# Two first weight tiles taken row by row, gate columns beside the last value columns, two query and key tiles inside memory attention

## The chip, the cores and the metric

The kernel runs on one core of a Trainium2 chip. A time is the device time of one execution in microseconds (us); lower is better. The engines are named as the profile names them: PE is TensorE (matmuls and transposes; PEld its weight loads), ACT is ScalarE, DVE is VectorE, POOL is GpSimd, SP is SyncE, which here only issues transfers (DMA). Each engine works through its own instructions in order and waits at semaphores for the others.

## The reference, cut to what matters

Two layers of a transformer on 512 tokens of width 1024, each a mixer with memory attention beside it and then a convolutional feed-forward block. The change lies in the projections of the first layer, whose mixer is gated linear attention (GLA):

```python
xn = rmsnorm(h, norm_mix[i])                       # x * rsqrt(mean(x*x) + eps) * gain
mem_kv = rmsnorm(mem, norm_mem[i]) @ w_mem_kv[i]   # 256 memory tokens
q, k, v, g, lr, mq = split_cols(xn @ gla_w_in[i], GLA_SIZES)   # 384, 384, 768, 768, 16, 256
log_a = jax.nn.log_sigmoid((lr @ gla_w_gate_up[i] + gla_b_gate[i])) / GLA_GATE_NORM
main = gla_mixer(q, k, v, log_a, g, gla_out_norm[i])
mo = mem_attention(mq, mem_kv)
h = h + jnp.concatenate([main, mo], axis=-1) @ w_out[i]
```

The 16 columns of lr are the gate columns: the decays log_a come from them.

## The kernel before

Activations lie transposed: the 1024 features are eight tiles (k = 0 to 7) of 128 partitions by 512 tokens. Every number is carried as a high and a low part (xh, xl; wh, wl; Qh, Ql), and each product is three matmuls: high by high, low by high, high by low. The high part is written by ScalarE (L277, L280 or L263), the low part, a difference, by VectorE (L278, L281 or L264). Weights come in tiles of 128 by 1024 (512 KB) over SyncE's queue (L243) into a pool of three buffers (wraw), and their parts into pools of three (wh, wl).

The row scale (the rsqrt of the mean square) isn't put on x. Projections take x times gain, and the scale is multiplied in afterwards. It is made of eight squares (ACT) summed on VectorE (sqacc, L332), a sum over partitions on TensorE (L338), a small VectorE step (rc, L348), a power on GpSimd (L349), and four transposes (L355) that spread it over partitions; ScalarE copies it out (rb, L359). For the memory tokens the same is done under names with m: rows mt (three buffers), parts mh and ml, sums sqaccm, scale rcm and rbm.

The order of the first layer before. The first key tile (glak[0]) comes in two halves, between rows of x. It is multiplied as rows arrive (L525), 24 matmuls, and between them stand three groups of fp32 matmuls (L530, `small`) that make the 16 gate columns of the raw rows. Then come the first query tile and the second key tile (glaq[0], glak[1]; L299), with the row scale inside the second. The gate rows are added and scaled on VectorE (L591, L592, L594), split (L595), and turned to decays by 8 matmuls of 384 columns (L605). The decays la are copied over partitions by two pairs of transfers (lad<-la, L615). Three more query and key tiles follow.

Then the memory keys (`mem_kv`): two projections of 256 columns, memory values, keys copied so that each head lies twice over the partitions (mt and mkd from mkf, L375), and split to mK (L380, L381). Two query tiles of memory attention (glamq) follow; each is scaled (sq, L400), copied by head (qd, L375), and split to Qh and Ql (L277, L278). In memory attention (`mem_att`) the scores sc (L454), the softmax and the transposes of each 128 queries stand between pieces of the GLA value projection, which fill TensorE: eight value tiles, four with 512 columns and four with 256.

The program is written with a tile layer that orders the instructions of each engine; `behind` adds an order between two instructions. Where it stands, the order of an engine isn't that of the source alone.

## Time and profile before

| what | value |
|---|---|
| median of three runs | 1259.99 us (1258.33 to 1260.75) |
| the profiled execution | 1260.37 us, span 1258.6 us |
| granted TensorE clock, mean | 0.999 |
| TensorE busy | 1248.6 us, 99% of the span |
| VectorE busy | 816.4 us, 65% |
| ScalarE busy | 605.5 us, 48% |
| the chain that ended last | TensorE 91%, DMA 3%, DVE 3%, ACT 2% |

The span goes from the first to the last instruction on the core. A timeline row gives start, duration, engine, line, operation, output and inputs, the partitions by elements and the count; in brackets stands how long the engine was idle ahead of it, and what ended that. Matmul durations overlap, so the distance between starts is the price of one.

### The profile page before, as it was taken

To read this page: it belongs to the slowest core of one execution; us is meant where nothing else is said; L and a number is where in the kernel's file an instruction comes from. 1 tells how busy PE (TensorE), PEld (TensorE's weight loads), DVE (VectorE), ACT (ScalarE), POOL (GpSimd) and SP (SyncE) were. 2 spreads that over 40 slices of the span, in tenths; PEclk is the share of its full clock that TensorE was granted. 3 is DMA by queue.
4 is the path that set the end of the run, shared out by engine and by line. 5 is a ranking of instruction groups with operands and counts; after the bars stand their busy time and mean duration, and the time that the engine had idled before them with its cause. 6 is when DMAs were issued, how large, how long until landed. Compare 5 with 4: busy or idle time off the path is not lost.

```text
span 1258.6 us, 18412 instructions
## 1 busy us (share of the span) xinstructions
PE 1248.6 (99%) x7054; PEld 1043.6 (83%) x7054; DVE 816.4 (65%) x1380; ACT 605.5 (48%) x1136; POOL 119.0 (9%) x144
## 2 busy tenths in 40 slices
PE   9999999999999999999999999999999999999998
PEld 6888889888888888888888788888888888888887
DVE  7756886577777774334677877855777777773331
ACT  7546654454444443223455677763544444442231
POOL 1000000000000000000102366650000000000000
PEclk9999999999999999999999999999999999999999
DMA  7651112343333333333766432303233333333321
GB/s 246 159 164 62 34 42 77 93 119 94 92 99 101 101 90 95 101 101 93 211 177 183 128 112 79 104 10 99 85 101 101 95 92 99 101 105 89 95 84 68
DMA packets 44891, 131.53 MB, mean 105 GB/s; under 512 B 6036, under 2 KB 11702, under 8 KB 44804
## 3 DMA queue, kind: packets, MB, share of 16 engines
q1 hardware_dynamic: 43124, 128.64, 35.3%
q10 hardware_dynamic: 1680, 1.72, 0.5%
q8 instruction: 56, 0.92, 0.3%
q14 instruction: 31, 0.25, 0.1%
HBM read 116.13 MB, written 2.15 MB: 94 GB/s over the span
## 4 chain that ended last, share of the span: by engine, by line
PE 91%; DMA 3%; DVE 3%; ACT 2%; issue 1%; SPq 0%; ACTq 0%; POOL 0%; POOLq 0%; DVEq 0%
PE acc L299 41%; PE acc L958 17%; PE acc L894 6%; PE po L1256 3%; PE acc L680 3%; PE acc L1256 3%; PE sc L1256 2%; PE pt L1257 2%; PE acc L1027 2%; PE acc L1170 2%; PE po L317 2%; PE sc L894 1%; DMA wraw<-in_wp 1%; PE pt L746 1%; PE acc L317 1%
## 5 line engine op out<-in xcount | busy, mean ns | idle before, releaser
L264 DVE TENSOR_TENSOR wl<-wraw,wh 128x1024 fp32r<-128x1024 f32 x180 | 229.3, 1274 | 139.8 <-ACT wh L263 137.3
L299 PE MATMUL acc<-xh,wh 128*128 128x512 f32 x792 | 308.9, 390 | 0.0
L299 PE MATMUL acc<-xl,wh 128*128 128x512 f32 x792 | 308.2, 389 | 0.0
L299 PE MATMUL acc<-xh,wl 128*128 128x512 f32 x792 | 307.0, 389 | 0.0
L263 ACT ACTIVATE wh<-wraw 128x1024 fp32r<-128x1024 f32 x180 | 190.8, 1060 | 226.7 <-PE acc L958 75.0
L299 PEld LDWEIGHTS acc<-xh,wh 128*128 128x128 f32 x792 | 148.7, 188 | 31.6 <-ACT sq L328 0.9
L299 PEld LDWEIGHTS acc<-xl,wh 128*128 128x128 f32 x792 | 148.7, 188 | 31.0
L299 PEld LDWEIGHTS acc<-xh,wl 128*128 128x128 f32 x792 | 148.7, 188 | 30.5
L958 PE MATMUL acc<-ah,wh 128*128 128x512 f32 x308 | 119.8, 389 | 0.0
L958 PE MATMUL acc<-ah,wl 128*128 128x512 f32 x308 | 119.8, 389 | 0.0
L958 PE MATMUL acc<-al,wh 128*128 128x512 f32 x308 | 119.8, 389 | 0.0
L939 DVE TENSOR_TENSOR u<-acc,rb 128x512 f32<-128x512 f32 x88 | 60.5, 688 | 73.7 <-PE acc L299 69.1
L277 ACT ACTIVATE ah<-hc 128x512 fp32r<-128x512 f32 x44 | 27.8, 632 | 117.1 <-DVE hc L946 117.1
L941 ACT ACTIVATE hc<-u,vec 128x512 f32<-128x512 f32 x88 | 71.1, 808 | 2.7 <-DVE u L939 2.0
L943 DVE SCALAR_TENSOR_TENSOR hc<-u,vec,hc 128x510 f32<-128x510 f32 x88 | 66.0, 750 | 3.0
L958 PEld LDWEIGHTS acc<-al,wh 128*128 128x128 f32 x308 | 57.8, 188 | 12.1
L945 ACT ACTIVATE hc<-hc 128x512 f32<-128x512 f32 x44 | 27.8, 632 | 83.1 <-DVE hc L943 83.0
L958 PEld LDWEIGHTS acc<-ah,wl 128*128 128x128 f32 x308 | 57.8, 188 | 12.0
L958 PEld LDWEIGHTS acc<-ah,wh 128*128 128x128 f32 x308 | 57.8, 188 | 11.9
L942 DVE SCALAR_TENSOR_TENSOR hc<-u,vec,hc 128x511 f32<-128x511 f32 x88 | 65.5, 744 | 1.8 <-ACT hc L941 1.8
L1335 POOL TENSOR_TENSOR P<-P,ssm 128x256 f32<-128x256 f32 (+3 forms) x48 | 63.3, 1339 | 1.8
L1327 ACT ACTIVATE P<-P,smn 128x128 f32<-128x128 f32 (+3 forms) x96 | 53.3, 558 | 6.6 <-DVE smn L1325 6.0
(407 smaller groups left out, 2107.4 us busy)
## 6 DMA issues: line engine op xcount, KB each, us to landing
wraw<-in_wp SPq DMA_DIRECT2D x197, 512.0 KB, 3.6
strip<-vecd SPq DMA_DIRECT2D x12, 448.0 KB, 4.1
qd<-qf SPq DMA_DIRECT2D x24, 128.0 KB, 2.4
h<-in_xT SPq DMA_DIRECT2D x8, 256.0 KB, 5.2
mt<-in_memT SPq DMA_DIRECT2D x16, 128.0 KB, 3.5
kd<-kf SPq DMA_DIRECT2D x16, 128.0 KB, 2.4
lad<-la SPq DMA_DIRECT2D x4, 384.0 KB, 7.5
qd<-sq SPq DMA_DIRECT2D x12, 128.0 KB, 2.8
```

The lines of the kernel that those rows point to most:

```text
L263: self.made = nc.scalar.activation(wh, raw, AF.Copy)
L264: self.left = nc.vector.tensor_tensor(out=wl, in0=raw, in1=wh.bitcast(F32), op=ALU.subtract)
L299: self.last = self.nc.tensor.matmul(ps[:M, :N], u[:, M * k:M * k + M], x[k][i][:, :N], start=n == 0, stop=n == 23)
L894: self.nc.tensor.matmul(ps[:, cols], a[:, o], b[:, cols], start=start and i == 0 and k == ks[0], stop=stop and k == 5 and i == 2)
L939: nc.vector.tensor_tensor(out=u, in0=ps, in1=rb, op=ALU.mult)
L941: nc.scalar.activation(c, u, AF.Identity, scale=tap(2), bias=tap(3))
L942: nc.vector.scalar_tensor_tensor(out=c[:, 1:], in0=u[:, :S - 1], scalar=tap(1), in1=c[:, 1:], op0=ALU.mult, op1=ALU.add)
L943: nc.vector.scalar_tensor_tensor(out=c[:, 2:], in0=u[:, :S - 2], scalar=tap(0), in1=c[:, 2:], op0=ALU.mult, op1=ALU.add)
L958: nc.tensor.matmul(ps, a[:, o], x, start=n == 0, stop=n == 3 * NJ - 1)
L1256: mm = lambda *args, **kw: pe(nc.tensor.matmul(*args, **kw))
L1327: nc.scalar.activation(P[:, br, :n], P[:, br, :n], AF.Exp, scale=-1.0, bias=mn[:, br:br + 1], accum_out=f[:, j, br:br + 1])
L1335: nc.gpsimd.tensor_tensor(out=P, in0=P, in1=f[:, i, :].unsqueeze(2).to_broadcast([128, 2, 128 * t + 128]), op=ALU.mult)
```

## The change

**Head.** The first key tile and the first query tile both come as halves between the rows of x, and each row, once split, is multiplied with both tiles (`begin`, 48 matmuls in a fixed order). The gains of the first norm come as 8 by 128 numbers and are turned by a transpose among the warm-up matmuls; the load of `wlr` and the early load of 64 columns of `vec` are gone. The gate matmuls (`small`) are gone.

**Gate columns.** The 16 gate columns of the weights stand beside the last 256 value columns: four chunks "glavg" of two blocks of 272 columns. They are multiplied right after the third tile, 96 matmuls of 272 columns, with the row scale inside them (sums after the fifth step of three matmuls, transposes after the tenth). The gate columns then lie by tokens; they are scaled, turned by four transposes and made to decays inside the fourth query and key tile.

**Order.** The memory keys and queries follow at once. Of the values only the 512 first columns are left for memory attention, and the last two query and key tiles follow them as its filling.

```diff
-    moving("glav", gw, ar(1280, 1536), 4)
+    both = np.concatenate([ar(1280, 1536), ar(2304, 2320)])
+    a = _blocks(gw, both, 272).reshape(128, 4, 544)
+    for c in range(4):
+        add("glavg", np.concatenate([a[:, c], np.zeros((128, 480), a.dtype)], axis=1))
...
+        self.first = self.const.tile([128, 152], F32, tag="first", name="first")[:, 24:32]
         self.vec = self.t(self.const, [128, V_N], "vec")
-        self.gains = self.t(self.const, [128, 64], "gains")
+        gT = self.t(self.tmp, [128, S], "rb", bufs=1)[:8, :128]
         self.h = [self.t(self.keep, [128, S], f"h{k}") for k in range(KC)]
         row = lambda eng, k: eng.dma_start(self.h[k], I["xT"][128 * k:128 * k + 128, :])
-        self.raw = self.t(self.wraw, [128, 1024], "wraw")
-        part = lambda c: nc.sync.dma_start(self.raw[:, 512 * c:512 * c + 512], I["wp"][self.W["glak"][0]][:, 512 * c:512 * c + 512])
+        self.raw = [self.t(self.wraw, [128, 1024], "wraw") for _ in range(2)]
+
+        def part(n, c):
+            c = slice(512 * c, 512 * c + 512)
+            nc.sync.dma_start(self.raw[n][:, c], I["wp"][self.W[("glak", "glaq")[n]][0]][:, c])
+
         row(nc.sync, 0)
-        nc.scalar.dma_start(self.gains, I["vec"][:, :64])
-        nc.scalar.dma_start(self.wlr, I["wlr"])
-        part(0)
+        nc.scalar.dma_start(gT, I["gT"])
+        part(0, 0)
         row(nc.sync, 1)
-        part(1)
-        for k in range(2, KC):
+        part(1, 0)
+        row(nc.sync, 2)
+        row(nc.sync, 3)
+        part(0, 1)
+        row(nc.sync, 4)
+        part(1, 1)
+        for k in range(5, KC):
             row(nc.sync, k)
...
-        for _ in range(10):
-            nc.tensor.matmul(idle[:, :128], self.ones, self.ones, start=True, stop=True)
+        warm = lambda: nc.tensor.matmul(idle[:, :128], self.ones, self.ones, start=True, stop=True)
+        for _ in range(5):
+            last = warm()
+        turned = nc.tensor.transpose(idle[:, 128:136], gT, self.ident[:8, :8])
+        self.behind(turned, last)
+        nc.vector.tensor_copy(self.first, idle[:, 128:136])
+        for _ in range(4):
+            self.behind(warm(), turned)
...
-    def mem_kv(self, l, keep):
+    def mem_kv(self, l, keep, banks="acc"):
...
-            pk = [self.ps("acc") for _ in range(2)]
+            pk = [self.ps(banks) for _ in range(2)]
             self.projA(pk[0], self.wget(self.W[f"memk{l}"][0]), N=MEM, x=mx, at={12: lambda: self.rms_sums(MEM, "m")})
-            self.projA(pk[1], self.wget(self.W[f"memk{l}"][1]), N=MEM, x=mx)
+            w = self.wget(self.W[f"memk{l}"][1])
+            if l == 0:
+                self.behind(self.made, self.rowed)
+            self.projA(pk[1], w, N=MEM, x=mx)
...
-+                ws = [[self.t(self.wsp, [128, 1024], tag, FR) for tag in ("wh", "wl")] for _ in range(2)]
+                first = []
+                splits = []
+                def chained():
+
+                    for ins, n in ((self.made, 0), (self.left, 1)):
+                        if splits:
+                            self.behind(ins, splits[0][n])
+                    splits[:] = [(self.made, self.left)]
+
+                def row(k):
                     self.split_x(0, [k])
...
+                    chained()
+
+                def halfw(n, c):
+                    c = slice(512 * c, 512 * c + 512)
+                    self.split_to(ws[n][0][:, c], ws[n][1][:, c], self.raw[n][:, c])
+                    chained()
+
+                def begin(*parts):
+
+                    for n, u, i, k in parts:
+                        ins = nc.tensor.matmul(qps[n], ws[n][u][:, 128 * k:128 * k + 128], self.x[k][i], start=k + u + i == 0, stop=k == KC - 1 and i == 1)
+                        if first:
+                            self.behind(ins, first[0])
+                        first[:] = [ins]
+
+                H, L, Wl = (0, 0), (0, 1), (1, 0)
+                A, B = ((lambda p, k, n=n: (n, *p, k)) for n in range(2))
+                row(0)
+                halfw(0, 0)
+                begin(A(H, 0), A(L, 0))
+                row(1)
+                begin(A(H, 1), A(Wl, 0), A(Wl, 1))
+                halfw(1, 0)
+                begin(B(H, 0), B(H, 1), A(L, 1), B(L, 0), B(L, 1))
+                row(2)
+                begin(A(H, 2), B(H, 2), B(Wl, 0), B(Wl, 1), A(Wl, 2), B(Wl, 2), A(L, 2), B(L, 2))
+                row(3)
+                begin(*(t(p, 3) for p in (H, Wl, L) for t in (A, B)))
+                halfw(0, 1)
+                row(4)
+                begin(A(H, 4), A(Wl, 4))
+                halfw(1, 1)
+                begin(B(H, 4), A(L, 4), B(L, 4), B(Wl, 4))
+                for k in range(5, KC):
+                    row(k)
+                    begin(*(t(p, k) for p in (H, Wl, L) for t in (A, B)))
+                self.sq_step(0, self.h[0], S, after=self.made)
+                third = self.wget(self.W["glak"][1])
...
-                for i in (1, 2):
-                    self.projA(qps[i], early[i - 1], late=i == 1, at=self.rms_at(6, 18) if i == 2 else ())
-                rc, rb = self.rc, self.rb
+                self.projA(qps[2], third, late=True)
...
-                nc.scalar.copy(lr[:16], ps[:16])
-                nc.vector.tensor_tensor(out=lr[:16], in0=ps[32:48], in1=lr[:16], op=ALU.add)
-                nc.vector.tensor_tensor(out=lr[:16], in0=ps[64:80], in1=lr[:16], op=ALU.add)
-                lrs = self.t(self.tmp, [128, S], "sq", FR, bufs=2)
-                nc.vector.tensor_tensor(out=lr[:16], in0=lr[:16], in1=rb[:16], op=ALU.mult)
-                nc.scalar.activation(lrs[:64], lr[:64], AF.Copy)
-                nc.vector.tensor_tensor(out=lrs[64:], in0=lr[:64], in1=lrs[:64].bitcast(F32), op=ALU.subtract)
-                for i in range(4):
-                    queries_keys(i)
+                lrs = self.t(pp, [128, S], "lr", FR)
+                nc.gpsimd.memset(lrs[:64].bitcast(F32), 1.0)
+                nc.gpsimd.memset(lrs[64:].bitcast(F32), 0.0)
+                lrT = self.t(pp, [128, 4, 16], "lrT")
+                pv = [self.ps(tag) for tag in ("po", "po", "sc", "pt")]
+                for n, _ in enumerate(self.stepsB("glavg", 0, 2, 272, pv, self.x)):
+                    if n == 4:
+                        bank = self.rms_sums(S, "")
+                    if n == 9:
+                        self.rms_rows(S, "", self.last, bank)
+                        rc, rb = self.rc, self.rb
+                for i in range(3):
+                    for _ in queries_keys(i, self.left):
+                        pass
+
+                def value(t):
+                    return nc.scalar.activation(v[:, t, 512:], pv[t][:, :256], AF.Copy, scale=rc[:, t:t + 1])
+
+                for t in range(4):
+                    nc.vector.tensor_scalar_mul(lrT[:, t], pv[t][:, 256:272], rc[:, t:t + 1])
+                for t in range(2):
+                    value(t)
                 la = self.t(pp, [128, 4, 384], "la")
                 lad = self.t(pp, [128, 4, 2, 384], "lad")
                 pz = []
-                for c in range(4):
-                    z = self.ps("pt" if c >= 2 else "po")
+
+                def rows():
+
+                    pb = self.ps("po")
+                    for t in range(4):
+                        self.behind(nc.tensor.transpose(pb[:16, 128 * t:128 * t + 128], lrT[:, t], self.ident), self.last)
+                    self.rowed = nc.scalar.activation(lrs[:16], pb[:16], AF.Copy)
+                    for t in range(2, 4):
+                        self.behind(value(t), self.rowed)
+                    nc.vector.tensor_tensor(out=lrs[64:80], in0=pb[:16], in1=lrs[:16].bitcast(F32), op=ALU.subtract)
+
+                def decay(c):
+
+                    z = self.ps(("po", "po", "acc", "pt")[c])
                     for i, g in enumerate(gus):
-                        nc.tensor.matmul(z[:, :384], lrs[:97, 128 * c:128 * c + 128], g, start=i == 0, stop=i == 1)
+                        self.behind(nc.tensor.matmul(z[:, :384], lrs[:97, 128 * c:128 * c + 128], g, start=i == 0, stop=i == 1), self.last)
                     nc.scalar.activation(la[:, c, :], z[:, :384], AF.Abs)
                     pz.append(z)
+
+                at = {13 + 3 * c: lambda c=c: decay(c) for c in range(4)}
+                at[4] = rows
+                for _ in queries_keys(3, None, at):
+                    pass
...
-                for i in (4, 5):
-                    queries_keys(i)
...
-                    mK, mV = self.mem_kv(0, mk)
+                    mK, mV = self.mem_kv(0, mk, "sc")
...
-                            for g, (rows, N) in enumerate(((2, 512), (4, 256))):
-                                pv = [self.ps("acc" if t < 2 else "po") for t in range(4)]
-                                yield from self.stepsB("glav", 4 * g, rows, N, pv, self.x)
-                                for t in range(4):
-                                    nc.scalar.activation(v[:, t, 512 * g:512 * g + N], pv[t][:, :N], AF.Copy, scale=rc[:, t:t + 1])
+                            pv = [self.ps("acc" if t < 2 else "po") for t in range(4)]
+                            yield from self.stepsB("glav", 0, 2, 512, pv, self.x)
+                            for t in range(4):
+                                nc.scalar.activation(v[:, t, :512], pv[t], AF.Copy, scale=rc[:, t:t + 1])
+                            for i in (4, 5):
+                                yield from queries_keys(i)
...
-                            upto(6)()
+                            upto(6 if len(calls) < 5 else 9)()
```

On VectorE, this is where the row scale of x (rc) stands. Names with sqacc are the sums of x's squares, sqaccm and sqm those of the memory rows, mt, mh and ml the memory rows and their parts. Before:

```order
L332 TENSOR_TENSOR sqacc_215<-sqacc_215,sq_248 128x512
L264 TENSOR_TENSOR wl_406<-wraw_403,wh_405 128x1024
L348 TENSOR_SCALAR rc_290<-pt_281 128x4
L281 SCALAR_TENSOR_TENSOR ml_91_479<-mt_474,gains_83,mh_90_478 128x256
L332 TENSOR_TENSOR sqaccm_476<-sqaccm_476,sqm_484 128x256
```

After:

```order
L353 TENSOR_TENSOR sqacc_238<-sqacc_238,sq_265 128x512
L353 TENSOR_TENSOR sqaccm_536<-sqaccm_536,sqm_553 128x256
L298 SCALAR_TENSOR_TENSOR ml_106_557<-mt_551,vec_82,mh_105_556 128x256
L353 TENSOR_TENSOR sqaccm_536<-sqaccm_536,sqm_562 128x256
L298 SCALAR_TENSOR_TENSOR ml_110_566<-mt_560,vec_82,mh_109_565 128x256
L353 TENSOR_TENSOR sqaccm_536<-sqaccm_536,sqm_571 128x256
L298 SCALAR_TENSOR_TENSOR ml_114_575<-mt_569,vec_82,mh_113_574 128x256
L281 TENSOR_TENSOR wl_391<-wraw_388,wh_390 128x544
L353 TENSOR_TENSOR sqaccm_536<-sqaccm_536,sqm_580 128x256
L369 TENSOR_SCALAR rc_340<-pt_331 128x4
```

The row scale stood ahead of the first memory row; now it stands behind the sum of the sixth (sqm_580, from mt_578), whose buffer is that of the third (mt_551).

On TensorE, this is the start of memory attention, behind the last matmul of the second query tile. The names wh and wl with xh and xl are the value tile and x. Before:

```order
L317 MATMUL acc_799<-wh_805,xh_147 128x512
L317 MATMUL acc_799<-wl_806,xh_147 128x512
L317 MATMUL acc_799<-wh_805,xl_148 128x512
L317 MATMUL po_801<-wh_805,xh_147 128x512
L317 MATMUL acc_800<-wh_805,xh_147 128x512
```

Twenty-four such matmuls stood there ahead of the first score (sc). After:

```order
L479 MATMUL sc_893<-mK_148_714,Qh_169_848 128x256
L479 MATMUL sc_931<-mK_148_714,Qh_169_848 128x256
L479 MATMUL sc_893<-mK_148_714,Ql_170_849 128x256
L479 MATMUL sc_931<-mK_148_714,Ql_170_849 128x256
L338 MATMUL acc_859<-wh_865,xh_150 128x512
L338 MATMUL acc_860<-wh_865,xh_150 128x512
L338 MATMUL po_861<-wh_865,xh_150 128x512
L338 MATMUL po_862<-wh_865,xh_150 128x512
L479 MATMUL sc_893<-mK_150_720,Qh_172_855 128x256
L479 MATMUL sc_931<-mK_150_720,Qh_172_855 128x256
L338 MATMUL acc_859<-wl_866,xh_150 128x512
```

Six score matmuls stand ahead of most of the first value tile.

On SyncE, these are the transfers around the key copies (mt and mkd from mkf). The names lad are the decays' copies, and wraw_803 before and wraw_863 after are the first value tile that attention multiplies. Before:

```order
L615 DMA lad_377<-la_376 64x4x384 x2
L243 DMA wraw_752<-in_wp 128x1024
L243 DMA wraw_803<-in_wp 128x1024
L375 DMA mt_651<-mkf_647 64x256 x2
L375 DMA mt_657<-mkf_647 64x256 x2
```

After:

```order
L681 DMA lad_461<-la_460 64x4x384 x2
L397 DMA mt_711<-mkf_707 64x256 x2
L397 DMA mt_717<-mkf_707 64x256 x2
L397 DMA mt_723<-mkf_709 64x256 x2
L397 DMA mkd_729<-mkf_709 64x256 x2
L681 DMA lad_461<-la_460 64x4x384 x2
L260 DMA wraw_863<-in_wp 128x1024
L260 DMA wraw_907<-in_wp 128x1024
```

One pair of decay copies moved behind the key copies, and the first value tile behind both.

More of the change, by code (lines that the diff above doesn't have):

```diff
@@ L309, in stepsB @@
             ks = range(rows * c, rows * c + rows)
-            wh, wl = self.wget(self.W[name][first + c], gain, ks)
+            wh, wl = self.wget(self.W[name][first + c], gain, ks, rows * N)
             for r, k in enumerate(ks):
@@ L527, in small @@
-                def small(a, b, after):
-                    for n in range(a, b):
-                        o = 32 * ((n + 1) % 3)
-                        gate = nc.tensor.matmul(ps[o:o + 16], wlr[:, n], self.h[n], start=n < 3, stop=n >= 5)
-                        self.behind(gate, after)
-                    return gate
-                for k in range(KC):
-                    self.split_x(0, [k])
-                    if k < 2:
-                        c = slice(512 * k, 512 * k + 512)
-                        self.split_to(wh[:, c], wl[:, c], self.raw[:, c])
-                    gate = small(0, 2, last) if k == 1 else None
-                    for i in range(2):
-                        last = first(wh, k, i, start=k + i == 0, stop=False)
-                        if gate is not None:
-                            self.behind(last, gate)
-                    if k >= 2:
-                        first(wl, k - 2, 0, start=False, stop=False)
-                    if k == 4:
-                        small(2, 5, last)
@@ L548, in gla_layer @@
-                for k in (KC - 2, KC - 1):
-                    last = first(wl, k, 0, start=False, stop=k == KC - 1)
-                small(5, 8, last)
-                early = []
-                for r, (name, j) in enumerate((("glaq", 0), ("glak", 1))):
-                    for k in range(3 * r, 3 * r + 1 + 2 * r):
-                        self.sq_step(k, self.h[k], S, after=self.made)
-                    early.append(self.wget(self.W[name][j]))
-                    if not r:
-                        for k in (1, 2):
-                            self.sq_step(k, self.h[k], S, after=self.made)
+                ws = [[self.t(self.wsp, [128, 1024], tag, FR) for tag in ("wh", "wl")] for _ in range(2)]
@@ L559, in gla_layer @@
+                begin(A(H, 4), A(Wl, 4))
[6 more added lines that the diff above has]
+                third = self.wget(self.W["glak"][1])
                 nc.sync.dma_start(self.vec, I["vec"])
-                for k in range(6, KC):
+                for k in range(1, KC):
@@ L561, in gla_layer, with queries_keys @@
                     self.sq_step(k, self.h[k], S, after=self.made)
-                def queries_keys(i):
+                def queries_keys(i, after=None, steps=()):
                     j, r = divmod(i, 2)
```

52 lines of the change are left out of this document (25 added, 27 removed).

## The prediction

> **What bounds the kernel now.** I read the page first, then TensorE's waits, then the timeline of the first 80 us.
>
> ```profile
> span 1258.6 us, 18412 instructions
> PE 1248.6 (99%) x7054; PEld 1043.6 (83%) x7054; DVE 816.4 (65%) x1380; ACT 605.5 (48%) x1136; POOL 119.0 (9%) x144
> PE acc L525 <- ACT wh L277: 0.7, 1, 0.7
> PE sc L454 <- ACT Qh L277: 0.5, 1, 0.5
> ```
>
> TensorE (PE) is busy for 1248.6 of 1258.6 us, and its largest waits on others outside the first matmul are the last two rows (total, count, longest). A change can gain only by taking matmul time away or by starting the chain earlier, and anything for which TensorE must wait is paid in full. All that is moved lies before the end of memory attention, so I follow TensorE's clock from its first real matmul to the first one of memory attention.
>
> ```profile
> 5.83 0.50 PE L525 MATMUL acc<-xh,wh 128*128 128x512 f32 x1 [0.69 <-ACT wh L277]
> 11.46 1.05 PE L530 MATMUL po<-h,wlr 128*16 128x512 f32 x6
> 12.44 0.50 PE L525 MATMUL acc<-xh,wh 128*128 128x512 f32 x1
> 21.70 0.39 PE L299 MATMUL sc<-xh,wh 128*128 128x512 f32 x1
> 26.80 0.60 PE L355 MATMUL pt<-ident,rc 128*128 128x128 f32 x4
> 27.15 0.48 PE L299 MATMUL sc<-xh,wh 128*128 128x512 f32 x1
> 34.76 0.85 PE L605 MATMUL pt<-wg,sq 97*128 97x384 f32 x4
> 35.46 0.39 PE L299 MATMUL acc<-xh,wh 128*128 128x512 f32 x1
> 46.35 0.28 PE L299 MATMUL acc<-mh,wh 128*128 128x256 f32 x1
> 69.48 0.39 PE L317 MATMUL acc<-wh,xh 128*128 128x512 f32 x1
> 75.99 0.39 PE L454 MATMUL sc<-mK,Qh 128*128 128x256 f32 x1 [0.50 <-ACT Qh L277]
> 76.72 0.39 PE L454 MATMUL sc<-mK,Ql 128*128 128x256 f32 x1 [0.34 <-DVE Ql L278]
> ```
>
> Matmuls overlap, so their price is the distance between starts. From 35.46 to 46.35 stand 48 matmuls of 512 columns: 0.227 each. Four of 384 columns take 35.46 − 34.76 = 0.70, 0.175 each. That is 0.41 ns per column, so 272 columns are an estimated 0.126 and 256 columns 0.12. A gate group of three products takes 12.44 − 11.46 = 0.98. Four transposes take 0.35.
>
> **Head.** Before, 15.87 us pass from 5.83 to the third tile at 21.70: 48 × 0.227 = 10.9 of tile matmuls, three gate groups 2.95, and 2.0 of waiting for pieces. Now the gate groups are gone, both tiles' weights come as halves between the rows, and every row feeds six matmuls, more than its 0.7 us of arrival. I take 0.6 of waiting, so the third tile starts at about 17.15, 4.55 earlier. The 16 gate columns cost 96 × 0.0066 = 0.64 later, four turns of them 0.35. So matmul time falls by 2.95 − 0.99 = 1.96. The extra turn of the gains stands among warm-up matmuls and costs nothing while the first row is awaited.
>
> **Row scale.** TensorE would reach the four transposes of the row scale after the third tile (5.44), the sums (0.56) and 30 value matmuls (3.78), at 26.95. But on VectorE the row scale (rc) now stands behind the memory rows up to the sum of the sixth, whose load waits for one of three buffers.
>
> ```profile
> 7.17 0.63 ACT L277 ACTIVATE wh<-wraw 128x512 fp32r<-128x512 f32 x1 [0.58 <-DMA wraw<-in_wp]
> 7.86 4.10 ACT L280 ACTIVATE xh<-h,gains 128x512 fp32r<-128x512 f32 x6
> 13.60 1.23 DVE L264 TENSOR_TENSOR wl<-wraw,wh 128x1024 fp32r<-128x1024 f32 x1 [0.85 <-ACT wh L263]
> 17.27 1.10 DVE L332 TENSOR_TENSOR sqacc<-sqacc,sq 128x512 f32<-128x512 f32 x1
> 23.33 0.67 DVE L332 TENSOR_TENSOR sqacc<-sqacc,sq 128x512 f32<-128x512 f32 x1
> 23.93 1.21 DVE L264 TENSOR_TENSOR wl<-wraw,wh 128x1024 fp32r<-128x1024 f32 x1
> 25.17 0.16 DVE L348 TENSOR_SCALAR rc<-pt 128x4 f32<-128x4 f32 x1
> 25.25 0.47 DVE L281 SCALAR_TENSOR_TENSOR ml<-mt,gains,mh 128x256 fp32r<-128x256 f32 x1
> 25.64 0.41 DVE L332 TENSOR_TENSOR sqaccm<-sqaccm,sqm 128x256 f32<-128x256 f32 x1
> 16.52 1.30 POOL L587 CAST lev<-lr 128x512 fp32r<-128x512 f32 x1 [10.67 <-DMA lr<-in_c_lev]
> DMA to landing us min/median/max: 3.5/3.6/3.9
> DMA to landing us min/median/max: 2.0/3.5/4.0
> ```
>
> The last row of x was split by 11.96 (7.86 + 4.10). Two more half tiles at that pitch, 0.68 each, less the 0.58 that ScalarE waited, give 12.75. The third tile's residual (wl) started 1.64 behind that, so now at 14.4. From there to the end of the third memory row VectorE has one wide residual (about 1.15), seven sums at 0.60 (23.33 to 23.93), one of 97 partitions (0.5), two of 544 columns at an estimated 0.68, three memory residuals at 0.39 (25.25 to 25.64) and two memory sums at 0.34: 9.1, to 23.5. The sum at 17.27 took 1.10 instead of 0.67 beside GpSimd's cast, which happens again: +0.43, and I allow 0.3 for ScalarE's squares: 24.2. Then the sixth memory row is fetched. The last two rows are landings of memory rows: the three issued behind weights at 25 to 28 us, and all before 60 us. I take 2.6, between the minimum and the loaded case, because one weight tile is in flight ahead of it. Square, sum and hand-over are 0.95, and from rc to the transposes it takes 26.80 − 25.17 = 1.63. The transposes come at 29.4 (28.0 with every cover, 31 with a landing of 3.6 and more waiting). TensorE stalls 2.45 there, so whatever else I mis-sized in the head is absorbed.
>
> [...]
>
> **From there to memory attention.** Before, 42.68 us (69.48 − 26.80). Now six matmuls of the third tile (1.36) and the last two query and key tiles (10.89) are gone from it; 66 of the 96 value matmuls (8.33) and the turns (0.35) are in it: 39.1. Attention starts at 68.5, 0.97 earlier. Inside it, 96 value matmuls of 256 columns (11.4) give way to 48 of 512 (10.9): −0.53. The memory values now share banks with the decays; I allow +0.1 for that.
>
> **The start of attention.** Before, TensorE went from the last query tile into 24 value matmuls, 5.6 us of cover, and the scores stood behind them. Now four score matmuls stand first and wait for the first query pair, and the value tile's cast stands behind that pair on ScalarE. The cover is gone. The chain of waits there is this:
>
> ```profile
> 56.89 3.69 SPq L375 DMA_DIRECT2D mt<-mkf  x6
> 61.96 6.81 SPq L243 DMA_DIRECT2D wraw<-in_wp  x4
> 65.42 0.42 DVE L381 TENSOR_TENSOR mK<-mkd,mK 64x256 fp32r<-64x256 f32 x1 [1.25 <-ACT mK L380]
> 65.87 0.69 DVE L400 SCALAR_TENSOR_TENSOR sq<-acc,rb 128x512 f32<-128x512 f32 x1
> 66.65 2.47 ACTq L375 DMA_DIRECT2D qd<-sq  x4
> 73.22 0.63 ACT L277 ACTIVATE Qh<-qd 128x512 fp32r<-128x512 f32 x1 [6.07 <-DMA qd<-sq]
> 73.89 0.69 DVE L278 TENSOR_TENSOR Ql<-qd,Qh 128x512 fp32r<-128x512 f32 x1 [3.52 <-DMA qd<-sq]
> 75.31 0.63 ACT L277 ACTIVATE Qh<-qd 128x512 fp32r<-128x512 f32 x1 [0.50 <-DMA qd<-sq]
> DMA to landing us min/median/max: 2.3/5.9/6.1
> DMA to landing us min/median/max: 6.6/7.7/8.3
> q1 hardware_dynamic: 249, 0.89, 48.3%
> q10 hardware_dynamic: 304, 0.50, 33.1%
> ```
>
> The query waits for the last key (65.42), then is copied (66.65), and is split at 73.22: 7.35 from 65.87. The landing rows are those of the six query copies and of the four weight tiles issued from 61.96 on; the last two rows give the queues' packets, MB and share from 68 to 74 us (q1 is SyncE's, q10 ScalarE's). Now the key copies start about 1 to 1.4 earlier and the decays' first spread is ahead of them on SyncE, so I put the scaled query at 64.0, 1.9 earlier than 65.87 (62.96, where the query tile ends, at best; 64.5 if the last key comes as it did). In flight there are three weight tiles as before and now the decays' second spread too. Taking the same 7.35, the split starts at 71.35; at best, with the 2.3 us landing of the late copies, about 67.5, and at worst, with the spread's 0.75 MB ahead at half the drain rate, about 73.5. The trace's row under load is the nearest, so 71.35.
>
> TensorE then has: high parts at 72.0, two score matmuls; low parts at 72.7, two more; the value tile's high part at 71.35 + 0.63 + 1.05 = 73.05, four matmuls of 0.227; the second pair, 2.1 later than the first (75.31 − 73.22), at 74.1, two matmuls. It ends at 74.35, with six of 0.12 and four of 0.227 done since 68.5: 4.2 us of stall. The value tile itself, issued near 62.8 behind the key copies and the spread, lands by 69.4 to 70.5 with the 6.6 to 7.7 of its neighbours and stays in that shadow. Before there were 0.50 + 0.34. Net +3.4, up to +5.5 with the worst split; were the split early, the value tile's landing of 6.6 and its cast would still make the stall 1.5, net +0.7, and −0.8 is the end only if that tile is early too. The later steps of attention keep about their cover: nine 512-column matmuls (2.04) in place of eighteen of 256 (2.2).
>
> **Sum.** −0.97 − 0.53 + 0.1 + 3.4 = +2.0 against the profiled execution's 1260.37, which is 0.38 above the median of the three runs, 1259.99. On the median that is 1262.0. A measurement of this kernel can tell about 0.2% from no change, 2.5 us: faster is below 1257.5, slower above 1262.5. So I forecast no change that can be told, at its slow edge.
>
> **Rivals.**
> *A, faster:* the query copies land as the late ones do (2.3), the value tile within 5, so that no stall stands at attention (−0.84), and the sixth memory row lands in 2.0, with the transposes at 28.2 (−2.17 instead of −0.97). Then −2.17 − 0.53 + 0.1 − 0.84 = −3.4: 1256.6; with the transposes at 26.95 too, 1255.3. For it speaks that TensorE's clock has 4.55 in hand; against it that qd landed in 5.9 or more under load.
> *B, slower, where I say no change:* the query copies stand behind the decays' second spread and three weight tiles. If 1.5 MB is drained first at the 0.23 MB per us of that window (0.89 + 0.50 MB in 6 us), the first split starts at about 74 and the stall is 6.9: 1264.7. It decides when the split starts later than 71.9, only half a microsecond behind my value. For it: more is queued than before. Against it: q10 moved 0.50 MB while q1 moved 0.89, so the copies don't wait their turn.
> *C, the gate columns aren't nearly free:* 272 columns cost what 384 do (0.175). 66 × 0.049 = +3.2 behind the row scale: 1265.2. Against it, 256, 384 and 512 lie on one line.
>
> [...]
>
> **Chances.** My forecast 0.46, A 0.14, B 0.34, C 0.03, a row scale beyond 31 us 0.03. So faster 0.14, same 0.46, slower 0.40. The likeliest case's own range is 1259.5 to 1262.5. The range over the cases goes from near A, 1257.2, to beyond B, 1265.0.
>
> **What would show it.** In the changed kernel's trace: the third tile near 17; a wait of about 2.4 at the four transposes with rc behind a memory sum; 272-column matmuls 0.126 apart; attention's first scores waiting some 4 us for Qh. I am wrong if that wait is below 1 us or above 6, if rc comes before 26, or if a later step of attention waits over 1 us.

## The result, and the profile after

The changed kernel takes 1270.93 us (median of five, 1269.38 to 1273.06) where the kernel before takes 1259.64 beside it on the same chip (1258.33 to 1260.75): ratio 1.0091, 95% interval 1.0076 to 1.0105. It is slower by 11.3 us. I had said 1262.0, no change, with 1265.0 as the upper end. The executions profiled took 1270.96 and 1260.37.

The changed kernel's page, TensorE's waits, and its granted clock in stretches of 4 us (in a row of the last kind: the stretch, TensorE busy, loads, DVE, ACT, POOL, then the clock, 1.00 being full, the DMA share and GB/s):

```profile
PE 1251.2 (99%) x7041; PEld 1048.2 (83%) x7041; DVE 814.2 (64%) x1385; ACT 606.6 (48%) x1138; POOL 119.1 (9%) x144
PE sc L479 <- ACT Qh L294: 5.5, 1, 5.5
PE pt L377 <- POOL rc L370: 3.7, 1, 3.7
32.00:36.00 4.00, 3.72 (x22) 3.72 (x23) 3.91 (x8) 1.56 (x4) 0.23 (x1) 0.72 0.39 113
36.00:40.00 4.00, 4.00 (x30) 4.00 (x29) 3.17 (x4) 1.28 (x2) 0.00 (x0) 0.86 0.07 26
76.00:80.00 4.00, 1.02 (x3) 0.80 (x4) 0.79 (x2) 1.58 (x2) 0.00 (x0) 0.76 0.87 249
80.00:84.00 4.00, 4.00 (x12) 3.32 (x12) 3.75 (x4) 2.52 (x3) 0.00 (x0) 0.50 0.56 139
84.00:88.00 4.00, 4.00 (x17) 3.18 (x17) 0.40 (x1) 0.00 (x0) 0.00 (x0) 0.88 1.04 273
```

Two waits, 9.2 us, stand where the prediction had put its two. But busy time grew by 2.6 us although matmul work was taken away: behind each wait the clock falls, to 0.72 and 0.86 and then to 0.76, 0.50 and 0.88. In stretches of half a microsecond it reads 0.50 from 34 to 37 and from 78.5 to 84.5, half. So that makes (0.28 + 0.14) × 4 / 0.5 = 3.4 us at half speed behind the first wait, and (0.24 + 0.50 + 0.12) × 4 / 0.5 = 6.9 us at the second, of which some 0.9 lies in the wait itself. The page's mean clock of 0.995 beside 0.999 shows this only as four thousandths.

The timeline of the changed kernel's TensorE, which answers to the rows shown of before:

```profile
17.64 0.39 PE L319 MATMUL sc<-xh,wh 128*128 128x512 f32 x1
24.29 0.29 PE L338 MATMUL po<-wh,xh 128*128 128x272 f32 x1
24.41 0.28 PE L338 MATMUL po<-wl,xh 128*128 128x272 f32 x1
32.28 0.65 PE L377 MATMUL pt<-ident,rc 128*128 128x128 f32 x4 [3.67 <-POOL rc L370]
33.40 0.29 PE L338 MATMUL pt<-wh,xl 128*128 128x272 f32 x1
33.53 0.28 PE L338 MATMUL po<-wh,xh 128*128 128x272 f32 x1
33.80 0.43 PE L338 MATMUL po<-wh,xl 128*128 128x272 f32 x1
34.03 0.43 PE L338 MATMUL po<-wh,xh 128*128 128x272 f32 x1
73.04 0.39 PE L319 MATMUL acc<-xl,wh 128*128 128x512 f32 x1
78.98 0.79 PE L479 MATMUL sc<-mK,Qh 128*128 128x256 f32 x2 [5.55 <-ACT Qh L294]
124.90 1.94 PE L510 MATMUL pt<-mPT,mV 128*64 128x512 f32 x8
```

The third tile starts at 17.64. 272-column matmuls stand 0.126 apart at 24.3, but 0.23 apart from 33.80 to 37.2: half speed. Attention starts at 73.27 (73.04 and one matmul more), 3.8 later than before. Its last product starts at 124.90; in the kernel before the same one does at 114.15:

```profile
114.15 1.94 PE L485 MATMUL pt<-mPT,mV 128*64 128x512 f32 x8
```

So 10.75 us, the whole loss, is there when memory attention ends. It adds up from attention's start (+3.8), its first scores (about +4.9 net: a wait of 5.55 and some tenths, less the 0.84 of before), the slow clock behind them (about +2.4), and the prediction's −0.53 for the shorter filling; a tenth or two stay open.

ScalarE, VectorE and SyncE at the two places in the changed kernel:

```profile
19.12 0.42 ACT L346 ACTIVATE sqaccm<-mt 128x256 f32<-128x256 f32 x1 [1.75 <-DMA mt<-in_memT]
19.97 0.48 DVE L298 SCALAR_TENSOR_TENSOR ml<-mt,vec,mh 128x256 fp32r<-128x256 f32 x1 [1.41 <-ACT mh L297]
26.48 1.83 SPq L433 DMA_DIRECT2D mt<-in_memT  x3
30.00 0.42 ACT L349 ACTIVATE sqm<-mt 128x256 f32<-128x256 f32 x1 [2.98 <-DMA mt<-in_memT]
30.44 0.42 DVE L353 TENSOR_TENSOR sqaccm<-sqaccm,sqm 128x256 f32<-128x256 f32 x1 [1.90 <-ACT sqm L349]
30.79 0.15 DVE L369 TENSOR_SCALAR rc<-pt 128x4 f32<-128x4 f32 x1
66.68 1.28 SPq L681 DMA_DIRECT2D lad<-la  x2
68.06 3.99 SPq L260 DMA_DIRECT2D wraw<-in_wp  x3
69.05 0.69 DVE L422 SCALAR_TENSOR_TENSOR sq<-acc,rb 128x512 f32<-128x512 f32 x1
78.30 0.63 ACT L294 ACTIVATE Qh<-qd 128x512 fp32r<-128x512 f32 x1 [9.73 <-DMA qd<-sq]
```

ScalarE waits 1.75 for the first memory row, with squares of x behind it in its order, and VectorE is idle 1.41 for what comes of it. The sixth memory row is fetched from 26.48 and squared at 30.00; VectorE is idle for 1.90, and rc follows. And the scaled query of 69.05 is split at 78.30, 9.25 later.

### The profile page after: what moved, and what is told of

Its sections match the earlier page's. It is cut to its first block, busy times and chain, and to the rows that moved or that the text cites. A ratio compares the mean times of both kernels' runs of the same rounds, so it can differ in the third digit from the quotient of the medians.

```text
span 1269.2 us, 18404 instructions
## 1 busy us (share of the span) xinstructions
PE 1251.2 (99%) x7041; PEld 1048.2 (83%) x7041; DVE 814.2 (64%) x1385; ACT 606.6 (48%) x1138; POOL 119.1 (9%) x144
## 4 chain that ended last, share of the span: by engine, by line
PE 93%; DMA 2%; DVE 1%; issue 1%; ACT 1%; SPq 1%; POOL 0%; ACTq 0%; POOLq 0%; DVEq 0%
PE acc L319 42%; PE acc L1024 17%; PE acc L960 6%; PE po L1322 3%; PE acc L746 3%; PE acc L1322 3%; PE po L338 2%; PE sc L1322 2%; PE pt L1323 2%; PE acc L1093 2%; PE acc L1236 2%; PE acc L338 2%; PE sc L960 1%; PE pt L812 1%; DMA mt<-in_memT 1%
## 5 line engine op out<-in xcount | busy, mean ns | idle before, releaser
L281 DVE TENSOR_TENSOR wl<-wraw,wh 128x1024 fp32r<-128x1024 f32 (+1 forms) x181 | 229.3, 1268 | 133.8 <-ACT wh L280 131.3
L280 ACT ACTIVATE wh<-wraw 128x1024 fp32r<-128x1024 f32 (+1 forms) x181 | 190.0, 1051 | 222.7 <-PE acc L1024 75.0
```

What stands on the lines that cost most here:

```text
L280: self.made = nc.scalar.activation(wh, raw, AF.Copy)
L281: self.left = nc.vector.tensor_tensor(out=wl, in0=raw, in1=wh.bitcast(F32), op=ALU.subtract)
```

## Experiments

Two theories. *Waits and clock:* the loss is the two waits, and each also costs half speed for some us behind it. *Work elsewhere:* the slow stretches come from the 272- and 256-column matmuls or from the transfers, and the change costs something the waits don't show. "Before" is run beside each group: 1258.4 to 1259.1. Each run gives its median in us, the ratio to the kernel before, and in brackets the 95% interval of that ratio.

**Row scale first.** Memory rows from the fourth on are kept behind the row scale on VectorE:

```diff
                 self.split_to(mh, ml, mt, self.gain(2 + l, k))
+                if l == 0 and k >= 3:
+                    for ins in (self.added, self.left):
+                        self.behind(ins, self.rcop)
```

> Changed kernel, but on VectorE the memory rows from the fourth on (their sums and low parts) stand behind rc, the first step of the row scale. Theory (rc waits for the sixth memory row's landing, and the idle TensorE then loses half its clock for some 3.4 us): rc near 27 instead of 30.8, transposes near 28.8 instead of 32.28 with a wait below 0.5, granted clock 1.00 from 32 to 40, the start of memory attention's wait unchanged near 5.5; 3.6 + 1.5 = about 5 us off, 1266. Rival (the sum over x or the power on GpSimd is late by itself): the transposes stay beyond 31 and the time stays within 1 us of 1271. Rival (idle and clock are unrelated): about 3.5 off, 1267.4, with the clock still low after 33.

1269.9, 1.0088 of before (1.0071 to 1.0105). The wait at the transposes is 0.2, and the clock is full up to 40 us. But TensorE now stops at the turn of the gate columns. VectorE makes these only from 40.19 on, behind those memory rows and the low part of a weight tile; the row names ScalarE's copy beside them (a row of TensorE's timeline and one of the clock by stretches):

```profile
40.98 1.02 PE L659 MATMUL po<-ident,lrT 128*16 128x128 f32 x4 [2.32 <-ACT v L645]
40.00:44.00 4.00, 3.02 (x10) 2.31 (x11) 1.50 (x6) 2.80 (x6) 0.00 (x0) 0.58 0.56 173
```

It is a miss in size, 1269.9 for 1266: the wait that was hidden behind the first came forward, with a slow clock (0.58) of its own.

**Values first.** 24 value matmuls ahead of the first scores, their tile's cast on ScalarE ahead of the query's splits (`lead` is the last of the 24):

```diff
+                        early = self.wget(self.W["glav"][0])
...
+                    if eng is not None and m + qt == 0:
+                        self.behind(ins, lead)
```

> Changed kernel, but the first value tile's load and cast stand ahead of the decays' second spread and of the query split, and 24 value matmuls ahead of the first scores. Theory (the wait at the first scores is uncovered time of the query copies, and the clock falls behind it): the row scale's wait stays at 3.7; at attention TensorE waits 1 to 2 us for the value tile, the scores wait for nothing, the clock stays 1.00 from 76 to 90; about 7 us off, 1264. Rival (the copies are late because TensorE is: they move on with it): the scores still wait over 3 us behind the values and less than 3 us is gained, over 1268.

1270.52, 1.0094 (1.0079 to 1.0109): a miss. The wait of 5.5 became waits of 2.8, 0.8 and 0.7, each in two pieces of 1.6 at most, and the clock fell all the same (0.54 from 84 to 88).

**Both.** The two edits together.

> Both edits together: row scale ahead of the memory rows, values ahead of the scores. Theory: the two waits and the two slow stretches add up, so 5 + 7 = 12 us off: 1259, within 2 of the kernel before; attention starts near 68.5. If the waits feed one another (an earlier attention waits longer for the value tile, whose load hangs on the memory keys and not on TensorE), 1 to 3 us less is gained: 1260 to 1262.

1270.4, 1.0099 (1.0084 to 1.0114): a miss, with 2.1 at the gate turn and scattered waits at the scores, and a slow clock behind each (0.68 from 40 to 44, 0.50 from 84 to 88).

**The waits filled with work.** The changed kernel, with matmuls against a zero tile in place of the two waits: 26 of 272 columns ahead of the transposes, 22 of 512 ahead of the scores, whose results add nothing. The four score matmuls of the first 128 queries then stand ahead of the values.

```diff
+                        for _ in range(26):
+                            ins = nc.tensor.matmul(pv[0][:, :272], self.zero, self.x[0][0][:, :272], start=False, stop=False)
```

> Changed kernel with both waits left, but filled: 26 matmuls of 272 columns with a stationary of zeros (adding nothing) ahead of the row scale's transposes, 22 of 512 columns ahead of the first scores; all four score matmuls of the first 128 queries then stand ahead of the values. Theory (idle TensorE loses its clock): both steps still come as late as before, near 32.3 and 77 to 79, but the granted clock is 1.00 behind both, pitches 0.126 and 0.227 at once; 1.5 + 2.4 = 3.9 off, less 1.6 for the scores' second pair that now stands ahead of the values: 1268 to 1269. Rival (the clock falls for another reason, such as the transfers or the mix of matmuls): the clock falls at the same places as before and the time is 1271 to 1273.

1270.63, 1.0094 (1.0079 to 1.0109): between the two theories' times. At the first place two rows of TensorE's timeline and one of the clock by stretches settle it:

```profile
27.92 3.46 PE L644 MATMUL po<-xh,zero 128*128 128x272 f32 x26
31.42 0.65 PE L377 MATMUL pt<-ident,rc 128*128 128x128 f32 x4
32.00:36.00 4.00, 4.00 (x34) 4.00 (x33) 3.90 (x8) 2.01 (x4) 0.00 (x0) 1.00 0.39 128
```

The transposes come as late as ever behind VectorE's rc (1.5), but with TensorE busy the clock stays at 1.00 where it was 0.72; up to 70 us this kernel is 2.4 ahead of the changed one (0.9 of it from the earlier rc). So the wait makes the slow stretch, and not the columns. At the second place waits of 0.3 to 0.85 were left between the scores, and the clock fell there (0.86 and 0.71 from 76 to 84). At the end of attention 1.5 of the gain was left (123.44 for 124.90), at the end of the trace 0.5, and the medians show 0.3. Half a microsecond of the rest is a wait in the second layer's memory attention (0.48 at 718.5); the other half isn't shown.

**Row scale and gates first.** As the first, with the gate columns and two value copies ahead of the first memory-key cast and the last memory rows.

```diff
+            if l == 0:
+                self.behind(self.made, self.v1)
+                self.behind(self.left, self.lrts)
```

> Changed kernel with rc ahead of the fourth memory row, as in the first experiment, and the gate columns' scaling (lrT) and the first two value copies ahead of the first memory-key tile's cast and of the last two memory rows, which were what TensorE waited for there. Theory (each wait of 2 us or more also costs half the clock for some 3 us): no wait over 0.5 before attention, clock 1.00 up to there, attention starts near 68.4 instead of 73.3, its wait stays near 5.5 with a slow stretch behind it: 5 off, 1266. Rival (what is taken away there comes back as a longer wait for the queries, whose copies hang on the transfers and not on TensorE): the wait at attention grows to 8 or more, and the time stays within 2 of 1270.

1266.67, 1.0064 (1.0049 to 1.0079): as expected. No slow clock before attention is left (1.00 up to 68), and the wait of 5.7 for the query stands alone.

**Values first, cast behind the query copies.**

> Changed kernel with 24 value matmuls ahead of the first scores, the value tile's load behind the last key copy and its cast behind all four query copies on ScalarE (in the earlier form it stood between them and held three of them up by 2.4). Theory: the row scale's wait and its slow stretch stay, attention starts near 73.2, waits under 1 for the value tile and under 2.5 in all for the second query pair: 6 to 7 off, 1264 to 1265. If a scatter of short waits is enough to lose the clock: a slow stretch behind the scores costs 2.5 of that back, 1267. Rival (query copies late for the transfers ahead of them, so later when the value tile is put ahead of them): the scores wait over 4 and the time is over 1268.

1268.51, 1.0077 (1.0062 to 1.0093): a miss, 1.5 above the time with a slow stretch and 3.5 or more above the theory's. Waits of 1.3, 0.8 and 1.9 were left at attention in its trace, with a slow stretch behind them (0.50 and 0.68 from 84 to 92); its four executions lie far apart (1266.42 to 1270.59).

**The last two together: row scale, gates and values first.**

> The two edits of these two kernels together. Theory: the parts add up, 5 + 6.5 off: 1259 to 1260, the kernel before; if the query copies don't move with TensorE, 2 to 3 less: 1262.

1264.31 (1262.1 to 1265.81), 1.0048 (1.0031 to 1.0065): a miss by 2.3 even from the later of the two times. What is left in its trace, which is of the shortest of the four executions, is 1.6 and 1.1 at the first values. ScalarE's timeline there:

```profile
65.10 3.86 ACTq L397 DMA_DIRECT2D qd<-sq  x4
69.01 1.06 ACT L280 ACTIVATE wh<-wraw 128x1024 fp32r<-128x1024 f32 x1 [5.17 <-issue]
```

The value tile's cast starts when ScalarE has issued the four query copies, which takes 3.86.

**The decays' second spread later.** Behind the query copies, which on SyncE's queue put it behind two more value tiles.

> The kernel with both edits, and the decays' second spread behind the query copies and behind two more value tiles. Theory (the query copies take 8.5 us from their issue instead of 6.1 because the spread's 0.75 MB lie ahead of them in the same engines): they land 1.5 to 2.5 sooner, near 6 to 7, the scores wait under 0.7, 1 to 3 off against the kernel with both edits, 1257.5 to 1259. Rival (the copies share with whatever stands in the other queue, which now is two value tiles): landing stays at 8 or more and the time is the same.

1263.6, 1.0037 (1.0022 to 1.0052). The rival's landing came, 8.1 to 9.5, but the edit did only half of what it says: the spread stood behind two more tiles, yet its first transfer left at 64.52, ahead of the copies (66.05). So the copies still had the spread beside them, and three tiles, and this doesn't tell which held them. TensorE waits 2.34 for the value tile, and here, against the theory, the clock stays full behind it (TensorE's row, and one of the clock by stretches):

```profile
72.02 0.50 PE L338 MATMUL acc<-wh,xh 128*128 128x512 f32 x1 [2.34 <-ACT wh L280]
72.00:76.00 4.00, 3.69 (x15) 2.72 (x16) 1.82 (x2) 0.00 (x0) 0.00 (x0) 1.00 1.10 229
```

**The second value tile held back.**

> The last version but one (row scale, gate turns and 24 value matmuls put ahead as before), with the load of the second value tile held behind the first pair of query copies, and the decays' second spread behind that tile. Theory: the query copies share their way with whatever is in flight, and the first value tile is late for the same reason; with that tile alone in flight it lands 3 to 4 us after its issue and is cast by 68, so the wait ahead of the value matmuls (2.7 before) falls under 0.5, the query copies land in 3 to 5 us, the scores wait for nothing: about 2.5 us less than that version, 1261 to 1262 where it took 1264.3, and the profiled execution near or under the kernel before. Rival: the copies' 6 to 9 us are their own (64-partition copies, issue and hand-over) and nothing changes: 1264.

1263.49, 1.0039 (1.0026 to 1.0053). The edit did not do what it says: the second tile, on SyncE's queue, left at 63.4, ahead of the copies on ScalarE's (65.96). So it doesn't test the theory. ScalarE's issue took 5.11, the cast came right behind it at 71.12, and the wait was 2.8, with a slow clock behind it (0.77 and 0.81 from 72 to 80).

**One wait, put into the kernel before.** To price waits alone, the kernel before gets a stop in the middle of its last query tile: a spare matmul of 512 columns (`touch`), copies of its bank by ScalarE, a second spare one.

```diff
+                            touch()
+                            for _ in range(3):
+                                nc.scalar.activation(z, bank, AF.Copy)
+                            touch()
```

> The kernel before, with one wait put into the middle of the last query tile: a spare 512-column matmul, three ScalarE copies out of its bank, and a second spare matmul behind them, with everything else of TensorE held behind that. The wait is about 2.2 us. Theory: a wait under the 3.7 that showed a fallen clock leaves the clock at 1.00, so the tile goes on at 0.227 a matmul and the cost is 2.2 + 2 x 0.23 = 2.7. Rival (any wait of some size costs a slow stretch behind it): 0.43 a matmul for about 3.4 us, +1.6 more.

> The same with six copies: one wait of about 4.0 us. Theory: TensorE goes on at full clock for 1 to 2 us, then at half clock for some 3.4 us, which costs 1.7 more: 4.0 + 0.45 + 1.7 = 6.2 behind the tile. Rival (the slow stretches of the changed kernel come from something else there, the 272-column or 256-column matmuls or the transfers): no slow matmul, 4.5.

> The same total wait in four pieces of about 1.0 us, each ended by one spare 512-column matmul, so TensorE is busy for about a quarter of 5 us. Theory from the versions with scattered waits: the clock goes by the share of busy time in a stretch of some us and not by one unbroken wait, so it falls to half here too: 4.0 + 5 x 0.23 + 1.7 = 6.8 behind the tile. Rival (one unbroken wait alone counts): 0.227 a matmul throughout, 5.2.

> The kernel before with the wait in the last query tile made of two copies: about 1.35 us in one piece, where 1.94 was followed by eight matmuls at half clock and four pieces of 0.69 by none. Theory (it is the unbroken wait that counts, and its edge lies between the 1.6 that kept the clock in one version and 1.94): all matmuls behind it stay 0.227 apart, cost 1.35 + 0.45 = 1.8. Rival (the share of a stretch of about 3.4 us counts, and the four pieces escaped by their spare matmuls): a slow stretch of some 3.4 us, 1.6 more, as behind 1.94.

TensorE's timeline of the four, in the order three copies, six, four pieces, two; the first row of each ends the last wait, the others are the query tile's matmuls behind it:

```profile
46.48 0.63 PE L580 MATMUL pt<-xh 128*128 128x512 f32 x1 [1.94 <-ACT sq L587]
46.91 0.63 PE L299 MATMUL acc<-xl,wh 128*128 128x512 f32 x1
49.90 0.49 PE L299 MATMUL acc<-xh,wh 128*128 128x512 f32 x1
```

```profile
48.45 0.50 PE L580 MATMUL pt<-xh 128*128 128x512 f32 x1 [3.83 <-ACT sq L587]
49.02 0.62 PE L299 MATMUL acc<-xh,wh 128*128 128x512 f32 x1
49.45 0.63 PE L299 MATMUL acc<-xh,wl 128*128 128x512 f32 x1
52.43 0.39 PE L299 MATMUL acc<-xl,wh 128*128 128x512 f32 x1
```

```profile
48.70 0.50 PE L580 MATMUL pt<-xh 128*128 128x512 f32 x1 [0.69 <-ACT sq L587]
49.03 0.40 PE L299 MATMUL acc<-xl,wh 128*128 128x512 f32 x1
49.27 0.40 PE L299 MATMUL acc<-xh,wh 128*128 128x512 f32 x1
```

```profile
45.55 0.50 PE L580 MATMUL pt<-xh 128*128 128x512 f32 x1 [1.32 <-ACT sq L587]
45.89 0.39 PE L299 MATMUL acc<-xl,wh 128*128 128x512 f32 x1
46.12 0.40 PE L299 MATMUL acc<-xh,wh 128*128 128x512 f32 x1
```

One wait of 1.94 is followed by matmuls 0.43 apart from 46.48 to 49.9, one of 3.83 by the same from 49.02 to 52.4: 3.4 us each time, which costs 1.6 to 1.7. One of 1.32, and four of 0.69 with a spare matmul between, leave 0.23 apart. So for 3.83 the theory held but for the start, 0.6 behind the wait and not 1 to 2. For 1.94 my expectation of a full clock fell, and the pieces speak against my belief that the busy share decides. Each is a single execution, so none shows a threshold (the wait of 2.34 above kept the clock), and their times (1263.08, 1264.7, 1263.47, 1260.4) are not compared.

**Query copies on SyncE's queue.** The version with row scale, gates and values first, with the four copies issued there, behind the first value tile and the spread. Two things change with it: the second value tile's load stands behind the copies, and the cast of the first no longer waits for their issue.

```diff
+            if early and c == 1:
+                self.behind(self.loaded, self.qcopied)
...
-            self.copied = (eng or self.nc.sync).dma_start(dst[64 * r:64 * r + 64], src[lo:lo + 64])
+            self.copied = self.nc.sync.dma_start(dst[64 * r:64 * r + 64], src[lo:lo + 64])
```

> The version with row scale, gate turns and 24 value matmuls put ahead (it took 1264.3), with the four first query copies issued on SyncE's queue, behind the first value tile and the decays' second spread and ahead of the other value tiles, instead of on ScalarE's. Theory: what held the value tile's cast there was not its load but ScalarE's own issue of the four copies, 3.86 us from 65.10 to 68.96, with the cast right behind at 69.01. Then the cast comes when the tile has landed, near 66.8, the 1.6 and 1.1 of waiting for wh and wl at 68.1 to 71.4 go, and about 2.5 us are gained: near 1261.7. Rival: the tile itself lands late (its load issued at 62.01 with 6 us under load gives 68), and the waits stay over 1 us: 1263 to 1264.

1260.57, 1.0014 (1.0005 to 1.0023), better than either theory's time. But in the timeline of its VectorE and ScalarE

```profile
64.87 0.69 DVE L435 SCALAR_TENSOR_TENSOR sq<-acc,rb 128x512 f32<-128x512 f32 x1
68.17 1.06 ACT L280 ACTIVATE wh<-wraw 128x1024 fp32r<-128x1024 f32 x1 [3.78 <-DMA wraw<-in_wp]
72.71 0.63 ACT L294 ACTIVATE Qh<-qd 128x512 fp32r<-128x512 f32 x1 [3.48 <-DMA qd<-sq]
```

the cast moved from 69.01 to 68.17 only, and there it waits for its load. So ScalarE's issue held it in the one and the load's landing in the other, one right behind the other; what each of the three changes gave isn't told apart.

**The spread behind the copies, on that queue.**

> The same with the decays' second spread moved behind the four query copies, which here stand on the same queue, so the order holds. Theory: with one value tile and the copies alone in flight the copies land in 3 to 5 us instead of 7 to 8, the scores wait for nothing, and the time is that of the version with the spread ahead or up to 0.5 us less: 1261 to 1261.7. Rival: the later value tiles, now issued later, are late for the matmuls behind the scores, and up to 2 us come back there.

1259.72, 1.0009 (1.0000 to 1.0018), 1.3 better than I had said. The timeline of VectorE, ScalarE and TensorE:

```profile
64.78 0.69 DVE L435 SCALAR_TENSOR_TENSOR sq<-acc,rb 128x512 f32<-128x512 f32 x1
66.26 1.06 ACT L280 ACTIVATE wh<-wraw 128x1024 fp32r<-128x1024 f32 x1 [1.97 <-DMA wraw<-in_wp]
68.48 0.63 ACT L294 ACTIVATE Qh<-qd 128x512 fp32r<-128x512 f32 x1 [1.17 <-DMA qd<-sq]
76.81 0.38 PE L499 MATMUL sc<-mK,Qh 128*128 128x256 f32 x1 [1.36 <-ACT mP L507]
```

From scaled query to split it takes 3.70 where it took 7.84; only the spread's place differs. The value tile is cast 1.9 earlier too. What is left is 1.36 at the third group of scores, for the softmax of the first.

**First scores behind 15 value matmuls, second value tile ahead of the spread.** Nine matmuls more stand between the first scores and the next.

> The last version with the first scores behind 15 value matmuls instead of 24 (the query is split at 68.5 to 71.1 there, long before they come at 74.2) and the second value tile's load ahead of the decays' second spread. In the last version the third group of scores waited 1.36 for the softmax of the first, because three groups stood in a row. Theory: with 9 matmuls more between the first and the later groups this wait goes and no other takes its place, so 1.0 to 1.4 are gained: 1258.3 to 1258.7, level with the kernel before or just under it. Rival: the second value tile, issued at 68 and landing in about 5, is cast behind 74.4 where it is needed, and a wait of about 1 stands there instead: 1259.5.

1258.9, 0.9996 of before (0.9987 to 1.0005). That wait is gone; one of 0.45, for the second value tile, is left at attention, and 0.5 and twice 0.4 ahead of it. Attention's last product starts at 113.00, 1.15 earlier than in the trace of before, whose execution (1260.37) lies 1.3 above the 1259.09 that before took beside this run:

```profile
113.00 1.94 PE L532 MATMUL pt<-mPT,mV 128*64 128x512 f32 x8
```

With the waits away, the change costs nothing that can be told, and by the medians gains nothing either. Against the changed kernel's 1270.93 that is some 12 us less, and it is as good as the kernel before, not better.

## Why the prediction was wrong

*Right:* both places and what TensorE waits for there. The third tile came at 17.64 (17.15; by its own terms, 2.95 of gate groups and 1.4 less waiting, the sum should have said 4.35 earlier and 17.35); 272 columns take 0.126, so rival C was out; nothing later in attention waits over 1 us.

*The step that failed* is the sum itself: "anything for which TensorE must wait is paid in full" counted a wait at its own length. No term priced the clock behind it. That cost 1.5 us behind the transposes (15 matmuls of 272 columns, 0.1 us more each, from 33.80 to 37.2) and 2.4 behind the scores, 3.9 of the 8.7 by which the trace's +10.7 at the end of attention exceeds my +2.0. The slow stretches behind 1.94, 3.67 and 3.83 lasted 3.4 us each, and the 6.9 around the wait of 5.55 are twice that.

*The row scale* was put at 29.4 (31 at worst) and came at 32.28. The sixth memory row was issued from 26.48 on and not near 24.2: VectorE began the third tile's residual 0.6 later (15.00), and was then idle for 0.57 and 1.41, the second for the first memory row, where my sum had it always busy. The row's data were squared 3.5 later, not 2.6. The mechanism, VectorE's order, was the one forecast. This is 2.9 of the 8.7.

*The query split* was taken at 7.35 behind the scaled query and took 9.25. I had the trace's row under load and rival B, the copies behind the spread and three weight tiles, at 0.34 against it. On one queue the spread alone ahead of the copies takes 4.1 (7.84 and 3.70), so there B's mechanism is shown. Between two queues, as here, it isn't: the change's copies were 1.9 slower with the spread and three tiles beside them, but no version took these away alone. Against B I had put the trace of before, where 0.50 MB moved on ScalarE's queue while 0.89 moved on SyncE's; the split came 1.9 later all the same. The stall was 5.55 and some tenths where I had 4.2: about 1.5 of the 8.7. The rest, 0.4, stands between transposes and attention.

I also took the row scale's stall as harmless cover ("whatever else I mis-sized in the head is absorbed"). It was, but it also hid the gate turn's wait of 2.3, and a change that only removes the stall brings that forward.

What stays open: what decides whether the clock falls. It isn't the length alone, since one wait of 1.94 lost it and one of 2.34 kept it, each in a single execution. Short waits close together did cost it in two values-first versions (none over 1.6) and in the filled version (none over 0.85), while four of 0.69 in the kernel before did not. A clock that falls in some executions alone would explain why a version's runs spread by 3.7 us (1262.1 to 1265.81). Its four executions fit that, with mean clocks of 0.999, 0.999, 0.998 and 0.998 from the shortest to the longest; but in the version with the spread later the longest (1264.16) has the highest, 0.999 against 0.997.

## What to carry to other kernels

On an engine that is busy 99% of the time, price a new wait at its length and, where it is as long as those that lost the clock here (1.94 to 5.55), as a risk, about 1.7 more for the clock (3.4 us at half speed; behind 5.55 it was 6 us and about 2.4). One of 2.34 cost no clock here. When work is moved ahead of what covered a transfer, look first at what stands ahead of that transfer on its own queue, and at the engine that issues it (moving four copies, one spread and one weight tile in the queues took the time from 1264.31 to 1259.72 here). And take all waits of a chain away before judging a reordering, since one removed alone brought the next one forward (3.67 at the transposes went, 2.32 at the gate turn came).

## What was not expected of the hardware

A wait of 1.94 us in one piece halved the speed of the matmuls (0.43 apart for 0.23) for 3.4 us, at once; one of 3.83 only 0.6 after work had begun again; the change's 3.67 only 1.5 after; and behind its 5.55 the slow stretch lasted about 6. One of 2.34, another of 1.32, and 2.8 in four pieces with a matmul between left the speed full (0.23 apart behind the last two, a clock of 1.00 behind 2.34). Four DMA issues held ScalarE for 2.5 to 5.1 us (2.47 in the kernel before, 3.02 in the changed one, 3.86 and 5.11 in two versions); what made the difference was not tested.
